# Product-key FFN block on one core: key search cut into pieces between weight splits, all up-weight splits on VectorE, larger gate-map instructions, streamed tiles at the right end of SBUF

## The chip, the core and the metric

One core of a Trainium2 chip runs the whole program. The metric is the device time of one execution in microseconds. Before the change it is 1149.65 us, the median of 3 runs (1148.85 to 1151.61).

## What is computed

One hybrid decoder layer for 256 tokens of width 1024 in float32: GLA and sparse attention from one input projection, cross-attention into 256 memory tokens, and then a PEER feed-forward block with 16,384 experts, with RMSNorms between. The front (both attentions, up to about 300 us) keeps its order; the change lies in the PEER block:

```
q = h @ Wq                               # 8 heads, two half keys each
s1, s2 = q1 @ subkeys1, q2 @ subkeys2    # 128 keys each
top-16 of s1, top-16 of s2               # values and ids
top-16 of (s1[a] + s2[b])                # over the 16 x 16 pairs
gate = softmax(top-16 scores)
expert = id1[a] * 128 + id2[b]
out = sum over the chosen: gate * gelu(h . down[expert]) * up[expert]
```

The kernel computes it densely: for every token the Gelu of all 16,384 experts, times a gate map that is zero where an expert is not chosen. An expert chunk is 128 experts with one second-key id; there are 128 chunks.

## The kernel before, in words

**Numbers as pairs.** Matmuls in fp32r lose bits, so every operand is a pair, a rounded high half and the remainder as a low half. `split` (L133 to L136) makes it: ScalarE copies the high half, VectorE, or GpSimd where the caller passes `P`, subtracts. `mm3` (L150 to L152) is then three matmuls: high by high, high by low, low by high. `weights` (L138) streams one chunk of 128 x 1024 floats by a DMA that SP issues into `raw` (4 buffers), and splits it into `whi` and `wlo` (3 buffers each), all of the pool `stream`.

**Two halves of 64 chunks.** Each half has a way down and a way back (loop `hf`, L852). *Way down*, per chunk `jj`: `proj_t` streams the down weights, splits them, and 24 matmuls (256 wide) fill a PSUM bank `pj` (2 of them); ScalarE writes the Gelu to `gl` (L862). *Way back*, per pair of chunks: the up weights are split, VectorE multiplies Gelu by the gate map (`L877`, 256 wide), the product is split into `Gh` and `Gl` (256 wide each), and 48 matmuls (512 wide) add to the four `y` banks.

**Who subtracts.** GpSimd makes the low halves of chunks 0 to 23 of the first half's way down (`LO_AT` 24) and of the first four chunks of each way back (`jj < 4`); VectorE makes the others.

**Key search.** While the first chunks run, VectorE finds the two top-16 lists (`best`, L734 and on) and the top-16 of the pairs. Then the loop at L772 turns positions into ids, per token tile `t` and key `q`: `idf` (ids as bf16), `past`, `ab`, `abf`, then a 2048-wide comparison `eq` (L789), its product with the ids broadcast over the 16 candidates (L791), four halving sums (L794) and a copy (L796). `gates_exp` (at chunk `EXP_AT`, 24) puts the `Exp` of the gates on ScalarE, `gates_t` (at chunk `KEY_AT`, 28) turns ids and gates to keys by tokens, and splits the gates into three bf16 parts `gp`.

**Gate maps.** From chunk 30 (`W_AT`) of the first half and chunk 8 of the second, two maps of 8 tokens come after every second chunk, 32 in a half (`gate_map`, L825). A map is two comparisons, `OI` (1024 wide) and `OJ` (512), three products `J` (L841), 24 short bf16 matmuls into a bank `pn` (2 of them), and a copy into `W` on ScalarE (L848).

**Order.** Nothing of the order is written out by hand. The framework's scheduler orders each engine's queue by its own estimates; `tc.issue_after(x)` holds an instruction behind `x`. An engine then works its queue strictly in that order, and waits for semaphores where an input or a buffer is late.

Of the kernel before, what the change touches and what calls it, by code (L numbers as in the profile page):

```python
# [23 lines left out]
HALF = NJ // 2  # L24


LO_AT, EXP_AT, KEY_AT, W_AT = 24, 24, 28, 30
SIZES = (256, 256, 512, 512, 16, 512, 128, 128, 128, 128, 128, 128, 24)
OFF = [0]
for _n in SIZES:  # L30
# [52 lines left out]
def body(ctx: ExitStack, tc, a, out, dbg=None):  # L83
# [49 lines left out]

    def split(src, hi, lo, eng=None):
        S.activation(hi, src, AF.Copy)  # L135
        (eng or V).tensor_sub(lo, src, hi.bitcast(FT))  # L136

    def weights(src, c, n, eng=None):  # L138

        raw = stream.tile([128, c * n], FT, name="raw", tag="raw", bufs=4)  # L140
        nc.sync.dma_start(raw, src)
        hi = stream.tile([128, c * n], FR, name="whi", tag="whi", bufs=3)
        lo = stream.tile([128, c * n], FR, name="wlo", tag="wlo", bufs=3)
        split(raw, hi, lo, eng)
        return hi.rearrange("p (c n) -> p c n", c=c), lo.rearrange("p (c n) -> p c n", c=c)
# [555 lines left out]
    def large(p):  # L701
        return p.tile([128, HALF, T], FT, name="big", tag="big")
# [4 lines left out]
    gp = [rt.tile([128, T], BF, name=f"gp{i}") for i in range(3)]  # L707
# [65 lines left out]
    for t in range(2):  # L773
        idf = ra.tile([128, 16, 16], BF, name="idf", bufs=2)
        V.tensor_copy(idf, ids[:, t])
        id4 = idf.rearrange("p (h q) k -> p h q k", q=2)
        past = ra.tile([128, 8, 16], U32, name="past", bufs=2)
        V.tensor_scalar(past, pos[t], 128, -128, op0=OP.max, op1=OP.add)
        for q in range(2):
            ab = ra.tile([128, 8, 16], U32, name="ab", bufs=2)  # L780
            if q == 0:
                V.tensor_scalar(ab, pos[t], 4, None, op0=OP.logical_shift_right)
            else:
                V.tensor_scalar(ab, pos[t], 15, None, op0=OP.bitwise_and)
            abf = ra.tile([128, 8, 16], BF, name="abf", bufs=2)
            V.tensor_tensor(abf, ab, past, op=OP.subtract if q else OP.add)
            eq = ra.tile([128, 8, 256], BF, name="eq", bufs=2)
            eq4 = eq.rearrange("p h (a k) -> p h a k", a=16)
            V.tensor_tensor(eq4, i16[:, None].to_broadcast([128, 8, 16, 16]),  # L789
                            abf[:, :, None, :].to_broadcast([128, 8, 16, 16]), op=OP.is_equal)  # L790
            V.tensor_tensor(eq4, eq4, id4[:, :, q, :, None].to_broadcast([128, 8, 16, 16]), op=OP.mult)  # L791
            for w in (128, 64, 32, 16):
                o = eq[:, :, :w]
                V.tensor_tensor(o, o, eq[:, :, w:2 * w], op=OP.add)  # L794
            r_ = ra.tile([128, 128], FT, name="r_", bufs=4)
            V.tensor_copy(r_.rearrange("p (h k) -> p h k", h=8), eq[:, :, :16])  # L796
            keys.append(r_)
# [10 lines left out]
    def gates_t(ins):  # L808
        p, pg = pn(), pn()
        with tc.issue_after(ins):  # L810
            for t in range(2):
                TE.transpose(p[:, t * 128:(t + 1) * 128], keys[2 * t], ident)
                TE.transpose(p[:, 256 + t * 128:256 + (t + 1) * 128], keys[2 * t + 1], ident)
                TE.transpose(pg[:, t * 128:(t + 1) * 128], g16[:, t].rearrange("p h k -> p (h k)"), ident)
        V.tensor_copy(idxi, p[:, :T])
        V.tensor_copy(idxj, p[:, T:])
        V.tensor_copy(gf, pg[:, :T])
        rr = ra.tile([128, T], FT, name="rr")
        V.tensor_copy(gp[0], gf)
        V.tensor_sub(rr, gf, gp[0])  # L820
        V.tensor_copy(gp[1], rr)
        V.tensor_sub(rr, rr, gp[1])
        V.tensor_copy(gp[2], rr)
        show("gf", gf)

    def gate_map(hf, W, t0):

        ts_ = slice(t0, t0 + 8)

        def two(x, n):  # L830
            return x[:, ts_].rearrange("p (g t) -> p g t", t=2)[:, :, None, :].to_broadcast([128, 4, n, 2])

        OI = rt.tile([128, 4, 128, 2], BF, name="OI", bufs=2)
        V.tensor_tensor(OI, ii2[:, None].to_broadcast([128, 4, 128, 2]), two(idxi, 128), op=OP.is_equal)
        OJ = rt.tile([128, 4, 64, 2], BF, name="OJ", bufs=2)
# [15 lines left out]
    big1 = None  # L851
    for hf in range(2):  # L852
        gl = g_half[hf]
        W = None
        for jj in range(HALF):
            j = hf * HALF + jj
            if hf == 0 and jj == EXP_AT:
# [5 lines left out]
            first = W_AT if hf == 0 else 8  # L863
            if jj % 2 and jj >= first and jj < first + 32:
                if W is None:
                    if hf == 0:
                        route.close()
                        big1 = pool(ctx, "big1")
                    W = large(big0 if hf else big1)
                for i in (jj - first - 1, jj - first):  # L870
                    gate_map(hf, W, i * 8)
        for jj in range(0, HALF, 2):
            G, w = [], []
            for i in range(2):
                j = hf * HALF + jj + i
                w.append(weights(a["up"][:, j], 1, D, P if jj < 4 else V))
                V.tensor_mul(gl[:, jj + i], gl[:, jj + i], W[:, jj + i])  # L877
                Gh = rt.tile([128, T], FR, name="Gh", bufs=2)
                Gl = rt.tile([128, T], FR, name="Gl", bufs=2)
                split(gl[:, jj + i], Gh, Gl)  # L880
                G.append((Gh, Gl))

            for i, t in ((0, 0), (1, 0), (0, 1), (1, 1)) if j == NJ - 1 else ((0, 0), (0, 1), (1, 0), (1, 1)):
# [93 lines left out]
```

## Time and profile before

| what | value |
|---|---|
| device time, median of 3 runs | 1149.65 us (1148.85 to 1151.61) |
| the profiled execution's own time | 1149.48 us |
| its span | 1147.7 us |
| PE (TensorE) busy | 1097.7 us, 96% |
| DVE (VectorE) busy | 812.9 us, 71% |
| ACT (ScalarE) busy | 580.9 us, 51% |
| POOL (GpSimd) busy | 157.0 us, 14% |
| mean granted TensorE clock | 0.982 |

The profile shows one execution, times in us from the span's start. A tile is given by the program's name without its buffer number; L136 is line 136 of the kernel. In a timeline, `x5` folds five instructions into one row, and the bracket gives the idle time ahead of it and what ended it. The granted clock is TensorE's, as a share of its full speed of 2.4 GHz. Matmuls overlap, so TensorE's pace is read from start to start.

### The profile page before, as it was taken

The page shows a single profiled execution, that of the slowest core. Times are in us where ns is not written, and L with a number is a line of the kernel's source. Part 1 is how long each engine was busy: PE and PEld are TensorE (multiplying, and loading weights), DVE is VectorE, ACT ScalarE, POOL GpSimd, SP SyncE. Part 2 cuts the span into 40 slices and gives each one's busy share as a digit, 9 for nine tenths or more (in the row PEclk, how much of TensorE's full clock was granted, in tenths as well). Part 3 has the DMA queues.
Part 4 walks back from the last instruction along what each step waited for, and adds up shares of the span by engine and source line. Part 5 has one row for each costly group of instructions (what it writes and reads, how often), then busy time and mean ns, then how long its engine had stood idle before and what let it go on. Part 6 is the DMA issues. An engine that isn't in the chain of part 4 may idle for free.

```text
span 1147.7 us, 20900 instructions
## 1 busy us (share of the span) xinstructions
PE 1097.7 (96%) x8174; PEld 979.4 (85%) x8174; DVE 812.9 (71%) x1698; ACT 580.9 (51%) x938; POOL 157.0 (14%) x83
## 2 busy tenths in 40 slices
PE   6999999999899969999799999999999999999996
PEld 5877789898799969999688888899999998888885
DVE  5763677675599978888786555547888956555555
ACT  5444445554454435666445444546666545445444
POOL 3303300000468900000500000000000003000001
PEclk9999999999899979999899999999999999999999
DMA  7633225563545535444365555564444565655653
GB/s 263 216 95 108 74 93 184 182 186 109 184 133 183 163 115 154 140 146 146 99 196 185 190 191 186 185 185 150 145 147 143 171 194 183 192 184 186 190 193 129
DMA packets 53568, 186.48 MB, mean 162 GB/s; under 512 B 6820, under 2 KB 8253, under 8 KB 53086
## 3 DMA queue, kind: packets, MB, share of 16 engines
q1 hardware_dynamic: 53470, 185.16, 51.1%
q8 instruction: 64, 1.05, 0.4%
q14 instruction: 34, 0.28, 0.1%
HBM read 182.76 MB, written 2.11 MB: 161 GB/s over the span
## 4 chain that ended last, share of the span: by engine, by line
PE 84%; DVE 11%; POOL 1%; DMA 1%; issue 1%; ACT 1%; SPq 0%; ACTq 0%; POOLq 0%; DVEq 0%
PE pj L150 13%; PE pj L151 13%; PE pj L152 13%; PE y L151 10%; PE y L152 10%; PE y L150 10%; PE pn L847 4%; PE po L152 1%; PE po L151 1%; PE po L150 1%; POOL wlo L136 1%; DVE eq L791 1%; DVE eq L794 1%; PE po L516 1%; DVE ids L734 1%
## 5 line engine op out<-in xcount | busy, mean ns | idle before, releaser
L135 ACT ACTIVATE whi<-raw 128x1024 fp32r<-128x1024 f32 (+1 forms) x328 | 344.3, 1050 | 287.4 <-PE pj L151 183.0
L136 DVE TENSOR_TENSOR wlo<-raw,whi 128x1024 fp32r<-128x1024 f32 x276 | 337.6, 1224 | 133.2 <-ACT whi L135 132.1
L152 PE MATMUL pj<-xh,wlo 128*128 128x256 f32 x1280 | 365.8, 286 | 12.6 <-DVE wlo L136 10.9
L150 PE MATMUL pj<-xh,whi 128*128 128x256 f32 x1280 | 369.4, 289 | 1.0 <-ACT tok L277 0.5
L151 PE MATMUL pj<-xl,whi 128*128 128x256 f32 x1280 | 365.3, 285 | 0.0
L152 PEld LDWEIGHTS pj<-xh,wlo 128*128 128x128 f32 x1280 | 247.7, 194 | 15.2 <-DVE wlo L136 11.4
L150 PEld LDWEIGHTS pj<-xh,whi 128*128 128x128 f32 x1280 | 247.6, 193 | 3.8 <-issue 0.9
L151 PEld LDWEIGHTS pj<-xl,whi 128*128 128x128 f32 x1280 | 247.8, 194 | 1.6 <-issue 1.0
L136 POOL TENSOR_TENSOR wlo<-raw,whi 128x1024 fp32r<-128x1024 f32 (+1 forms) x52 | 137.7, 2655 | 783.4 <-ACT whi L135 771.3
L151 PE MATMUL y<-wlo,Gh 128*128 128x512 f32 x512 | 203.6, 398 | 7.9 <-POOL wlo L136 7.9
L152 PE MATMUL y<-whi,Gl 128*128 128x512 f32 x512 | 203.4, 397 | 0.0
L150 PE MATMUL y<-whi,Gh 128*128 128x512 f32 x512 | 203.3, 397 | 0.0
L135 ACT ACTIVATE Gh<-big 128x256 fp32r<-128x256 f32 x128 | 53.3, 418 | 188.9 <-PE y L151 174.3
L151 PEld LDWEIGHTS y<-wlo,Gh 128*128 128x128 f32 x512 | 96.9, 189 | 31.6 <-POOL wlo L136 8.3
L150 PEld LDWEIGHTS y<-whi,Gh 128*128 128x128 f32 x512 | 96.8, 189 | 23.3
L152 PEld LDWEIGHTS y<-whi,Gl 128*128 128x128 f32 x512 | 96.8, 189 | 23.3
L136 DVE TENSOR_TENSOR Gl<-big,Gh 128x256 fp32r<-128x256 f32 x128 | 54.5, 427 | 77.6 <-ACT Gh L135 77.6
L841 DVE TENSOR_TENSOR J<-OJ,gp 128x512 bf16<-128x512 bf16 x192 | 74.9, 432 | 32.5 <-PE pn L847 32.5
L848 ACT ACTIVATE big<-pn 128x512 f32<-128x512 f32 x64 | 65.3, 1131 | 0.0
L877 DVE TENSOR_TENSOR big<-big 128x256 f32<-128x256 f32 x128 | 53.2, 466 | 3.3 <-ACT big L862 2.3
L847 PE MATMUL pn<-J,OI 128*128 128x64 bf16 x1536 | 52.1, 193 | 0.0
L847 PEld LDWEIGHTS <-OI 128*128 128x128 bf16 x1536 | 48.3, 97 | 1.4
(621 smaller groups left out, 1092.0 us busy)
## 6 DMA issues: line engine op xcount, KB each, us to landing
raw<-down_t SPq DMA_DIRECT2D x128, 512.0 KB, 3.8
raw<-up SPq DMA_DIRECT2D x128, 512.0 KB, 4.2
raw<-w_t SPq DMA_DIRECT2D x16, 512.0 KB, 4.4
raw<-xa_wk SPq DMA_DIRECT2D x8, 512.0 KB, 3.5
raw<-xa_wv SPq DMA_DIRECT2D x8, 512.0 KB, 3.8
raw<-w_out SPq DMA_DIRECT2D x8, 512.0 KB, 4.2
raw<-xa_wq SPq DMA_DIRECT2D x8, 512.0 KB, 3.9
raw<-xa_wo SPq DMA_DIRECT2D x8, 512.0 KB, 3.5
```

The costliest lines, as they stand in the source:

```text
L135: S.activation(hi, src, AF.Copy)
L136: (eng or V).tensor_sub(lo, src, hi.bitcast(FT))
L150: TE.matmul(o, lh, rh, start=start, stop=False)
L151: TE.matmul(o, lh, rl, start=False, stop=False)
L152: last["mm"] = TE.matmul(o, ll, rh, start=False, stop=stop)
L516: TE.matmul(pob[b][:, hd * 64:(hd + 1) * 64], pt_[:, i * 128:(i + 1) * 128], tok[:, k, b * 128 + g * 64:b * 128 + g * 64 + 64], start=k == ...
L734: V.max_index(ids[:, t, x, 8:], vals[:, t, x, 8:], s2_)
L791: V.tensor_tensor(eq4, eq4, id4[:, :, q, :, None].to_broadcast([128, 8, 16, 16]), op=OP.mult)
L841: V.tensor_tensor(J, OJ, two(gp[k], 64), op=OP.mult)
L847: TE.matmul(p[:, i], OI[:, g, :, q], Js[k][:, g, :, q], start=k == 0, stop=k == 2)
L848: S.activation(W[:, :, ts_].rearrange("p j t -> p t j"), p, AF.Copy)
L877: V.tensor_mul(gl[:, jj + i], gl[:, jj + i], W[:, jj + i])
```

## The change

1. **Key search in pieces.** GpSimd subtracts for chunks 0 to 19 only (`LO_AT` 20), and the search becomes a generator of 16 pieces. From chunk 20 on, each chunk issues one or two pieces, held behind the low half that was issued last, until chunk 32. `gates_exp` comes at chunk 21, `gates_t` at chunk 33 (`KEY_AT` 33). The ids are first written out 2048 wide by ScalarE (`rep`), so the product has two plain inputs.
2. **One J.** The three gate parts lie in one tile `gp` [128, T/8, 3, 8], and one product 1536 wide writes all three J's.
3. **Maps spread.** The 32 maps of a half are dealt out evenly, over 29 chunks from chunk 33 in the first half and over 54 from chunk 8 in the second. The first two maps of the second half are held behind the low half issued last.
4. **Way back.** VectorE splits all up weights. One product (512 wide) serves a pair of chunks and is held behind the low half issued last; `Gh` and `Gl` are one split of 512 per pair.
5. **Memory.** The pool `stream` moves to the right end of SBUF, with a margin of 8 floats behind it. The small `rstd` tiles have 2 buffers instead of 4.

The diff, cut to its core:

```diff
-LO_AT, EXP_AT, KEY_AT, W_AT = 24, 24, 28, 30
+LO_AT, KEY_AT = 20, 33
...
-    stream = pool(ctx, "stream")
+    edge = pool(ctx, "edge", side="right")
+    edge.tile([128, 8], FT, name="margin")
+    stream = pool(ctx, "stream", side="right")
...
-        (eng or V).tensor_sub(lo, src, hi.bitcast(FT))
+        last["lo"] = (eng or V).tensor_sub(lo, src, hi.bitcast(FT))
...
+    def key_pieces():
+        for t in range(2):
+            idf = ra.tile([128, 16, 16], BF, name="idf", bufs=2)
+            V.tensor_copy(idf, ids[:, t])
...
+                rep = ra.tile([128, 8, 256], BF, name="rep", bufs=2)
+                rep4 = rep.rearrange("p h (a k) -> p h a k", a=16)
+                S.activation(rep4, id4[:, :, q, :, None].to_broadcast([128, 8, 16, 16]), AF.Copy)
...
+                yield
...
-            V.tensor_tensor(eq4, eq4, id4[:, :, q, :, None].to_broadcast([128, 8, 16, 16]), op=OP.mult)
+                V.tensor_tensor(eq, eq, rep, op=OP.mult)
+                yield
...
-        Js = []
-        for k in range(3):
-            J = rt.tile([128, 4, 64, 2], BF, name=f"J{k}", bufs=2)
-            V.tensor_tensor(J, OJ, two(gp[k], 64), op=OP.mult)
-            Js.append(J)
+        J = rt.tile([128, 3, 4, 64, 2], BF, name="J", bufs=2)
+        parts = gp[:, t0 // 8].rearrange("p k (g t) -> p (k g) t", t=2)
+        V.tensor_tensor(J.rearrange("p k g j t -> p (k g) j t"),
+                        OJ.rearrange("p g j t -> p (g j t)")[:, None].to_broadcast([128, 3, 512]),
+                        parts[:, :, None, :].to_broadcast([128, 12, 64, 2]), op=OP.mult)
...
+            if hf == 0 and LO_AT <= jj < KEY_AT:
+                with tc.issue_after(last["lo"].ins):
+                    while done < 16 and done * (KEY_AT - 1 - LO_AT) < 16 * (jj + 1 - LO_AT):
+                        next(pieces)
+                        done += 1
+            first = KEY_AT if hf == 0 else 8
...
-                for i in (jj - first - 1, jj - first):
-                    gate_map(hf, W, i * 8)
+            while made < T // 8 and made * (HALF - 2 - first) < (T // 8) * (jj + 1 - first):
+
+                with tc.issue_after(last["lo"].ins) if hf and made < 2 else nullcontext():
+                    gate_map(hf, W, made * 8)
+                made += 1
...
-                w.append(weights(a["up"][:, j], 1, D, P if jj < 4 else V))
-                V.tensor_mul(gl[:, jj + i], gl[:, jj + i], W[:, jj + i])
...
+            with tc.issue_after(last["lo"].ins):
+                V.tensor_mul(g, g, v)
+            w = [weights(a["up"][:, hf * HALF + jj + i], 1, D, V) for i in range(2)]
+            G = [rt.tile([128, 2, T], FR, name=n, bufs=2) for n in ("Gh", "Gl")]
+            split(g, *G)
```

**VectorE at the key search.** Before, half of the search and the split behind it (`eq` comparison and product, `r_` the key, `wlo_4534` the low half of chunk 24; the four halving sums of L794 work on two tiles in turn):

```order
L791 TENSOR_TENSOR eq_3745<-eq_3745,idf_3724 128x2048
L794 TENSOR_TENSOR eq_3732<-eq_3732 128x8x128
L794 TENSOR_TENSOR eq_3745<-eq_3745 128x8x128
L794 TENSOR_TENSOR eq_3732<-eq_3732 128x8x64
L794 TENSOR_TENSOR eq_3745<-eq_3745 128x8x64
L794 TENSOR_TENSOR eq_3732<-eq_3732 128x8x32
L794 TENSOR_TENSOR eq_3745<-eq_3745 128x8x32
L794 TENSOR_TENSOR eq_3732<-eq_3732 128x8x16
L794 TENSOR_TENSOR eq_3745<-eq_3745 128x8x16
L796 CAST r__3739<-eq_3732 128x128
L796 CAST r__3752<-eq_3745 128x128
L136 TENSOR_TENSOR wlo_4534<-raw_4531,whi_4533 128x1024
```

Now, from the end of the top-16 (`g16`) on, with `wlo_4343`, `wlo_4392` and `wlo_4425` the low halves of chunks 20, 21 and 22:

```order
L773 TENSOR_TENSOR g16_3694<-top_3589 128x256
L138 TENSOR_TENSOR wlo_4343<-raw_4340,whi_4342 128x1024
L780 CAST idf_4372<-ids_3059 128x256
L783 TENSOR_SCALAR past_4374<-pos0_3590 128x128
L791 TENSOR_SCALAR ab_4378<-pos0_3590 128x128
L795 TENSOR_TENSOR abf_4380<-ab_4378,past_4374 128x128
L799 TENSOR_TENSOR eq_4382<-i16_3056,abf_4380 128x2048
L138 TENSOR_TENSOR wlo_4392<-raw_4389,whi_4391 128x1024
L802 TENSOR_TENSOR eq_4382<-eq_4382,rep_4376 128x2048
L138 TENSOR_TENSOR wlo_4425<-raw_4422,whi_4424 128x1024
L806 TENSOR_TENSOR eq_4382<-eq_4382 128x8x128
```

The search, two keys at a time in one block before, now goes one key at a time with a split after every piece or two, and the split of chunk 20 stands ahead of it.

**ScalarE at the same place.** `whi_4342`, `whi_4391`, `whi_4424`, `whi_4462` are the high halves of chunks 20 to 23; the rows of L878 are Gelus, `pj_4250` being chunk 17's and `pj_4346` chunk 20's:

```order
L137 ACTIVATE whi_4342<-raw_4340 128x1024
L878 ACTIVATE big_3048<-pj_4250 128x256
L788 ACTIVATE rep_4376<-idf_4372 128x2048
L878 ACTIVATE big_3048<-pj_4282 128x256
L137 ACTIVATE whi_4391<-raw_4389 128x1024
L788 ACTIVATE rep_4492<-idf_4372 128x2048
L878 ACTIVATE big_3048<-pj_4314 128x256
L137 ACTIVATE whi_4424<-raw_4422 128x1024
L137 ACTIVATE whi_4462<-raw_4460 128x1024
L878 ACTIVATE big_3048<-pj_4346 128x256
L814 ACT_TABLE_LOAD
L814 ACTIVATE g16_3694<-g16_3694 128x256
```

Two copies of 2048 (`rep`) and the `Exp` with its two table loads now stand among the high halves of chunks 20 to 23; the load back for the next Gelu follows the high half of chunk 24. Before, `Exp` stood at chunk 24.

**VectorE at the first turn.** Before, behind the last map's J and OI, up to the first up-weight split that VectorE makes (`wlo_7080`):

```order
L841 TENSOR_TENSOR J1_8785<-OJ_8781,gp1_3048 128x512
L841 TENSOR_TENSOR J2_8787<-OJ_8781,gp2_3049 128x512
L834 TENSOR_TENSOR OI_8815<-ii2_3050,idxi_3045 128x1024
L877 TENSOR_TENSOR big_3044<-big_3044,big_4808 128x256 x3
L136 TENSOR_TENSOR Gl_6993<-big_3044,Gh_6992 128x256
L136 TENSOR_TENSOR Gl_7004<-big_3044,Gh_7003 128x256
L877 TENSOR_TENSOR big_3044<-big_3044,big_4808 128x256 x18
L136 TENSOR_TENSOR Gl_7039<-big_3044,Gh_7038 128x256
L877 TENSOR_TENSOR big_3044<-big_3044,big_4808 128x256 x8
L136 TENSOR_TENSOR Gl_7050<-big_3044,Gh_7049 128x256
L877 TENSOR_TENSOR big_3044<-big_3044,big_4808 128x256
L136 TENSOR_TENSOR wlo_7080<-raw_7077,whi_7079 128x1024
```

Now, with `wlo_6838` the last down chunk's low half and `wlo_6871`, `wlo_6877`, `wlo_6912`, `wlo_6918` those of the first four up chunks:

```order
L854 TENSOR_TENSOR J_6775<-OJ_6773,gp_3051 128x1536
L138 TENSOR_TENSOR wlo_6838<-raw_6835,whi_6837 128x1024
L138 TENSOR_TENSOR wlo_6871<-raw_6868,whi_6870 128x1024
L901 TENSOR_TENSOR big_3048<-big_3048,big_4882 128x512
L138 TENSOR_TENSOR Gl_6881<-big_3048,Gh_6880 128x512
L901 TENSOR_TENSOR big_3048<-big_3048,big_4882 128x512
L138 TENSOR_TENSOR wlo_6877<-raw_6874,whi_6876 128x1024
L138 TENSOR_TENSOR Gl_6922<-big_3048,Gh_6921 128x512
L901 TENSOR_TENSOR big_3048<-big_3048,big_4882 128x512
L138 TENSOR_TENSOR wlo_6912<-raw_6909,whi_6911 128x1024
L138 TENSOR_TENSOR wlo_6918<-raw_6915,whi_6917 128x1024
```

The 18 and 8 products in a row are gone: products of 512 stand one at a time behind splits, and the splits of the first four up chunks have come to VectorE.

## Rows read from the trace of the kernel before

**Rows 1.** Table of stretches, all engines (first line: its columns).

```profile
core 0: us, PE busy (x) PEld busy (x) DVE busy (x) ACT busy (x) POOL busy (x), PEclk, DMA share, GB/s
400.00:420.00 20.00, 8.15 (x60) 7.75 (x60) 20.00 (x33) 5.69 (x8) 4.46 (x2) 0.75 0.21 61
500.00:520.00 20.00, 20.00 (x274) 19.87 (x273) 16.85 (x33) 13.03 (x18) 0.00 (x0) 1.00 0.52 149
```

**Rows 2.** TensorE's timeline, 397 to 424 us (start, us, engine, line, op, tiles, idle before).

```profile
397.33 0.39 PE L152 MATMUL pj<-xh,wlo 128*128 128x256 f32 x1 [0.38 <-POOL wlo L136]
...
401.71 0.39 PE L152 MATMUL pj<-xh,wlo 128*128 128x256 f32 x1 [1.25 <-POOL wlo L136]
...
407.45 0.28 PE L151 MATMUL pj<-xl,whi 128*128 128x256 f32 x1
...
418.33 0.58 PE L152 MATMUL pj<-xh,wlo 128*128 128x256 f32 x1 [10.60 <-DVE wlo L136]
...
423.57 0.28 PE L152 MATMUL pj<-xh,wlo 128*128 128x256 f32 x1
```

**Rows 3.** VectorE's timeline, the key search, and J in the map stretch.

```profile
390.52 8.90 DVE L791 TENSOR_TENSOR eq<-eq,idf 128x2048 bf16<-128x2048 bf16 x2
...
406.55 0.28 DVE L775 CAST idf<-ids 128x256 bf16<-128x256 uint32 x1
...
407.56 2.35 DVE L789 TENSOR_TENSOR eq<-i,abf 128x2048 bf16<-128x2048 bf16 x2
409.84 4.48 DVE L791 TENSOR_TENSOR eq<-eq,idf 128x2048 bf16<-128x2048 bf16 x2
...
417.06 3.48 DVE L136 TENSOR_TENSOR wlo<-raw,whi 128x1024 fp32r<-128x1024 f32 x3
...
542.14 1.09 DVE L841 TENSOR_TENSOR J<-OJ,gp 128x512 bf16<-128x512 bf16 x3
```

**Rows 4.** GpSimd's timeline, the last splits on the way down, and the turn.

```profile
383.42 2.54 POOL L136 TENSOR_TENSOR wlo<-raw,whi 128x1024 fp32r<-128x1024 f32 x1 [0.48 <-ACT whi L135]
386.30 18.16 POOL L136 TENSOR_TENSOR wlo<-raw,whi 128x1024 fp32r<-128x1024 f32 x5 [0.34 <-ACT whi L135]
...
561.24 10.73 POOL L136 TENSOR_TENSOR wlo<-raw,whi 128x1024 fp32r<-128x1024 f32 x1 [3.42 <-ACT whi L135]
```

**Rows 5.** TensorE's timeline, the turn.

```profile
563.51 0.40 PE L152 MATMUL y<-whi,Gl 128*128 128x512 f32 x1
563.74 0.39 PE L150 MATMUL y<-whi,Gh 128*128 128x512 f32 x1
572.02 0.79 PE L151 MATMUL y<-wlo,Gh 128*128 128x512 f32 x1 [7.89 <-POOL wlo L136]
...
577.22 0.40 PE L151 MATMUL y<-wlo,Gh 128*128 128x512 f32 x1
```

**Rows 6.** ScalarE's timeline, 388 to 411 us.

```profile
388.04 1.06 ACT L135 ACTIVATE whi<-raw 128x1024 fp32r<-128x1024 f32 x1 [1.55 <-issue]
...
408.80 1.28 ACT L801 ACT_TABLE_LOAD   x1
410.10 0.42 ACT L801 ACTIVATE g<-g 128x256 f32<-128x256 f32 x1
```

**Rows 7.** TensorE's timeline, a pair of maps between two chunks.

```profile
502.54 1.63 PE L847 MATMUL pn<-J,OI 128*128 128x64 bf16 x48
504.01 0.36 PE L150 MATMUL pj<-xh,whi 128*128 128x256 f32 x1
504.21 0.28 PE L151 MATMUL pj<-xl,whi 128*128 128x256 f32 x1
```

**Rows 8.** Costliest groups (busy us, mean ns of one | idle before): maps and G.

```profile
L848 ACT ACTIVATE big<-pn 128x512 f32<-128x512 f32 x64 | 65.3, 1131 | 0.0
L135 ACT ACTIVATE Gh<-big 128x256 fp32r<-128x256 f32 x128 | 53.3, 418 | 188.9 <-PE y L151 174.3
L877 DVE TENSOR_TENSOR big<-big 128x256 f32<-128x256 f32 x128 | 53.2, 466 | 3.3 <-ACT big L862 2.3
```

More of the change, by code (lines that the diff above doesn't have):

```diff
@@ L154, in rstd_of @@
     def rstd_of(late, early):
-        b, v, r, q = (tmp.tile([128, 1], FT, name=f"r{i}", tag=f"r{i}", bufs=4) for i in range(4))
+        b, v, r, q = (tmp.tile([128, 1], FT, name=f"r{i}", tag=f"r{i}", bufs=2) for i in range(4))
         V.tensor_scalar(b, early, 1.0 / D, EPS, op0=OP.mult, op1=OP.add)
@@ L706, in body @@
     idxj = rt.tile([128, T], BF, name="idxj")
-    gp = [rt.tile([128, T], BF, name=f"gp{i}") for i in range(3)]
+    gp = rt.tile([128, T // 8, 3, 8], BF, name="gp")
     ii2 = rt.tile([128, 128, 2], BF, name="ii2")
@@ L772, in body @@
     keys = []
[L773 to L790, printed above, removed]
-            V.tensor_tensor(eq4, eq4, id4[:, :, q, :, None].to_broadcast([128, 8, 16, 16]), op=OP.mult)
[L792 to L797, printed above, removed]
@@ new lines, in key_pieces @@
+    def key_pieces():
+        for t in range(2):
+            idf = ra.tile([128, 16, 16], BF, name="idf", bufs=2)
+            V.tensor_copy(idf, ids[:, t])
+            id4 = idf.rearrange("p (h q) k -> p h q k", q=2)
+            past = ra.tile([128, 8, 16], U32, name="past", bufs=2)
+            V.tensor_scalar(past, pos[t], 128, -128, op0=OP.max, op1=OP.add)
+            for q in range(2):
+                rep = ra.tile([128, 8, 256], BF, name="rep", bufs=2)
+                rep4 = rep.rearrange("p h (a k) -> p h a k", a=16)
+                S.activation(rep4, id4[:, :, q, :, None].to_broadcast([128, 8, 16, 16]), AF.Copy)
+                ab = ra.tile([128, 8, 16], U32, name="ab", bufs=2)
+                if q == 0:
+                    V.tensor_scalar(ab, pos[t], 4, None, op0=OP.logical_shift_right)
+                else:
+                    V.tensor_scalar(ab, pos[t], 15, None, op0=OP.bitwise_and)
+                abf = ra.tile([128, 8, 16], BF, name="abf", bufs=2)
+                V.tensor_tensor(abf, ab, past, op=OP.subtract if q else OP.add)
+                yield
+                eq = ra.tile([128, 8, 256], BF, name="eq", bufs=2)
+                eq4 = eq.rearrange("p h (a k) -> p h a k", a=16)
+                V.tensor_tensor(eq4, i16[:, None].to_broadcast([128, 8, 16, 16]),
+                                abf[:, :, None, :].to_broadcast([128, 8, 16, 16]), op=OP.is_equal)
+                yield
+                V.tensor_tensor(eq, eq, rep, op=OP.mult)
+                yield
+                for w in (128, 64, 32, 16):
+                    o = eq[:, :, :w]
+                    V.tensor_tensor(o, o, eq[:, :, w:2 * w], op=OP.add)
+                r_ = ra.tile([128, 128], FT, name="r_", bufs=4)
+                V.tensor_copy(r_.rearrange("p (h k) -> p h k", h=8), eq[:, :, :16])
+                keys.append(r_)
+                yield
@@ L818, in gates_t @@
         rr = ra.tile([128, T], FT, name="rr")
[L819 to L823, printed above, removed]
+        g8, r8 = (x.rearrange("p (g t) -> p g t", t=8) for x in (gf, rr))
+        V.tensor_copy(gp[:, :, 0], g8)
+        V.tensor_sub(r8, g8, gp[:, :, 0])
+        V.tensor_copy(gp[:, :, 1], r8)
+        V.tensor_sub(r8, r8, gp[:, :, 1])
+        V.tensor_copy(gp[:, :, 2], r8)
         show("gf", gf)
@@ L846, in gate_map @@
             for k in range(3):
-                TE.matmul(p[:, i], OI[:, g, :, q], Js[k][:, g, :, q], start=k == 0, stop=k == 2)
+                TE.matmul(p[:, i], OI[:, g, :, q], J[:, k, g, :, q], start=k == 0, stop=k == 2)
         S.activation(W[:, :, ts_].rearrange("p j t -> p t j"), p, AF.Copy)
@@ L851, in body @@
     big1 = None
+    pieces, done = key_pieces(), 0
     for hf in range(2):
@@ L854, in body @@
         W = None
+        made = 0
         for jj in range(HALF):
             j = hf * HALF + jj
-            if hf == 0 and jj == EXP_AT:
+            if hf == 0 and jj == LO_AT + 1:
                 gates_exp(gelu.ins)
@@ L862, in body @@
             gelu = S.activation(gl[:, jj], p, AF.Gelu_apprx_tanh)
[L863 to L869, printed above, removed]
-                for i in (jj - first - 1, jj - first):
-                    gate_map(hf, W, i * 8)
-        for jj in range(0, HALF, 2):
-            G, w = [], []
-            for i in range(2):
-                j = hf * HALF + jj + i
-                w.append(weights(a["up"][:, j], 1, D, P if jj < 4 else V))
-                V.tensor_mul(gl[:, jj + i], gl[:, jj + i], W[:, jj + i])
[L878 to L883, printed above, removed]
+            if hf == 0 and LO_AT <= jj < KEY_AT:
[3 more added lines that the diff above has]
+                        done += 1
@@ new lines, in body @@
+            first = KEY_AT if hf == 0 else 8
+            if jj < first:
+                continue
+            if W is None:
+                if hf == 0:
+                    route.close()
+                    big1 = pool(ctx, "big1")
+                W = large(big0 if hf else big1)
+            while made < T // 8 and made * (HALF - 2 - first) < (T // 8) * (jj + 1 - first):
+                with tc.issue_after(last["lo"].ins) if hf and made < 2 else nullcontext():
+                    gate_map(hf, W, made * 8)
+                made += 1
@@ new lines, in body @@
+        for jj in range(0, HALF, 2):
+            g, v = gl[:, jj:jj + 2], W[:, jj:jj + 2]
+            with tc.issue_after(last["lo"].ins):
[3 more added lines that the diff above has]
+            split(g, *G)
+            end = hf and jj == HALF - 2
+            for i, t in ((0, 0), (1, 0), (0, 1), (1, 1)) if end else ((0, 0), (0, 1), (1, 0), (1, 1)):
@@ L887, in body @@
                     n = slice(f * 512, (f + 1) * 512)
-                    mm3(y[t][f], G[i][0][:, s], G[i][1][:, s], w[i][0][:, 0, n], w[i][1][:, 0, n], j == 0, j == NJ - 1)
+                    mm3(y[t][f], G[0][:, i, s], G[1][:, i, s], w[i][0][:, 0, n], w[i][1][:, 0, n],
+                        j == 0, j == NJ - 1)
         if hf == 0:
```

## The prediction, made before the changed kernel was run

> **What bounds the kernel now.** I read four views in turn. The table of stretches comes first: in a normal stretch of the PEER loop TensorE is busy all 20 us at a granted clock of 1.00, but from 400 to 420 us only 8.15 of 20, at 0.75 [rows 1]. TensorE's timeline shows why: its last matmul before a hole starts at 407.45, and the next, at 418.33, is the first that needs the low half of chunk 24, which VectorE makes; two shorter waits, 0.38 and 1.25 us, were for GpSimd's low halves [rows 2]. Then the engines waited for. VectorE searches the keys without a break until 417.06 and only then splits chunk 24. The first half of the search runs beside GpSimd's splits, and there the two `eq` products take 8.90 us, against 4.48 in the second half, when GpSimd is done [rows 3]. GpSimd pays too: its last five splits take 18.16 us, where one took 2.54 before [rows 4]. At the turn to the way back one GpSimd split takes 10.73 us, beside a row of VectorE's products, and TensorE waits from 563.74 to 572.02 [rows 4, 5]. Elsewhere in the PEER part TensorE's own matmuls set the pace, so a lighter VectorE there is worth nothing by itself.
>
> **What the two holes cost.** Normally 47 steps take 401.71 to 407.45, 0.12 us each, so 24 matmuls, a chunk, take 2.88. First hole: 418.33 − 407.45 − 0.12 = 10.76 us of gap. Then the matmuls run at the lower of the clock's two levels, 1.2 GHz: the 24 steps from 418.33 to 423.57 take 5.24 us for 2.88, so 2.36 more. The two waits ahead are 0.38 and 1.25, and some 0.2 each for the restart (the stalled matmul lasts 0.39, a normal one 0.28, and the step after it is longer too). Together **15.2 us** [rows 2]. Second hole: a step is 0.23, so 572.02 − 563.74 − 0.23 = 8.05 us, and 12 steps to 577.22 take 5.20 for 2.8: **10.4 us** [rows 5]. That is 25.6 us, all that the change can win here.
>
> **The change part by part.**
> *Key search in pieces, LO_AT 24 to 20, KEY_AT 28 to 33.* GpSimd gives up chunks 20 to 23 and is done before 390, so the search no longer shares with it. VectorE's new order has the split of chunk 20 ahead of the search, so it stands idle from the end of the top-16 until ScalarE has made that chunk's high half, 388.04 + 1.06 = 389.1 [rows 6]. I count nothing for that; the room below pays it. Half of the search took 417.06 − 406.55 = 10.5 us alone. Its two products were 4.48 of that; both inputs are plain rows now (ScalarE writes `rep` out), so I price two between `is_equal`'s 2.35 and 4.48, at the first, which also reads plain rows of bf16: 8.4 us a half, 16.8 in all (21 at the other end) [rows 3]. The 13 splits of chunks 20 to 32 take 13 × 1.23 = 16 us (at most: three take 3.48) [rows 3], the gate sums 1.1. That is 34 us (38) in the 42 from 389.1 to TensorE's end of chunk 32: TensorE starts chunk 18 at 388.04, when the high half of chunk 20 may be written, so chunk 23 at 402.4 and chunk 33 at 431.2. A low half can be ready 5.76 − 1.06 − 1.23 = 3.5 us before its chunk, and no two splits have over 2.4 us of search between them (3.4 at the other end). So the first hole closes at either price.
> ScalarE gets four `rep` of 2048. Nearest row: 1.06 us for 1024 from SBUF, so 2.0; the other end, by the copy out of PSUM (1.13 for 512 [rows 8]), 4.5. The first two come right ahead of `Exp` and its table loads. Adding up ScalarE's order from 390.6, when `idf` is there: 2 × 2.0 for `rep`, 3 × 1.0 for high halves, 3 × 0.4 for Gelu (as `Exp`, also 256 wide) make 398.8; with load and `Exp` 1.70, a high half, the load back 1.28 and a Gelu, chunk 21's Gelu ends at 403.2 [rows 6]. TensorE wants that PSUM bank for chunk 23 at 402.4: **+0.8 us**, less than the 1.25 us after which the matmuls still kept their step. At the other end it is 5.8 us here and 2.5 at the second pair. The Trainium skill ("ScalarE: Activation LUTs", What ACT_TABLE_LOAD costs) counts a drain of about 1.38 us with each load. The trace has the load at 408.80 for 1.28 us and `Exp` at 410.10 [rows 6]: no drain. By the rule two loads would add 2.8 us here, and the sum would be 1130.6.
> *VectorE splits all on the way back; products in pairs, each held behind the last split.* The 26 products in two rows that stood ahead of the splits are gone from the order. At the turn the last map is copied to W within 1.7 us of TensorE's start of chunk 62 (high half, Gelu and 1.13 for the copy). Then product, high and low half of the first pair, at most two old ones each (0.93, 0.84, 0.93 [rows 8]): 4.4 us, against the 5.76 until the way back begins. So the second hole closes, with 1.3 us to spare. Steady: two splits 2.5, product and low half 1.9, 4.4 of the 24 × 0.23 = 5.6 us that a pair takes TensorE. That is the cover; if it is gone, each us more costs a us a pair.
> *One J for three, 512 to 1536.* Three took 1.09 us; one saves two starts, some 0.9 [rows 3]. VectorE's time, for which nobody waits: 0. Other end 1.68 us, at the old product's 1.09 ns an element (rival 1).
> *Maps spread.* First half: 32 maps in 29 chunks instead of 32; second: in 54. The matmuls are the same, but nearly every map now stands alone between chunks: 61 returns to the fp32r stream in place of 32 (three pairs remain). After a pair of maps the step from the first fp32r matmul to the next is 504.21 − 504.01 = 0.20 us, normally 0.12 [rows 7]: 0.08 × 29 = **+2.4 us**. At the start of the maps the first J follow the gate values so closely that TensorE waits some tenths at maps 1, 2 and 3: **+0.7** (0 to 1.5).
> *Streamed tiles at the right end, two `rstd` buffers for four.* In the front the order on every engine and its waits stay; no row shows an address to matter: 0. SP issues the same DMAs in the same order; 12 reloads wait for VectorE's split where they waited for GpSimd's.
>
> **Sum**, against the profiled execution's 1149.48 us (the runs' median is 1149.65, the same): 1149.5 − 15.2 − 10.4 + 0.8 + 2.4 + 0.7 = **1127.8 us**, my forecast.
>
> **Rivals.**
> 1. *J drops to one element a step.* VectorE then needs, per chunk of the first half, 1.23 + 1.1 × (2 × 0.36 + 0.36 + 1.68) = 4.3 us (`OI`, 1024 wide, as two J), 4.0 as starts overlap, against TensorE's 2.88 + 1.1 × (0.73 + 0.08) = 3.77 [rows 3, 7]: 0.25 × 29 = 7 us, **1135**. For: its operands are repeated over an outer dimension now. Against: inside they are the same pairs as before, and those ran at 0.36 us for 512. 0.07. The Trainium skill ("VectorE: DVE Perf Modes", Mode 2×_1P) asks for 16-bit data in unit steps; by that rule the rate stays.
> 2. *ScalarE falls behind*, `rep` at the PSUM copy's rate: 5.8 + 2.5 − 0.8 = 7.5 more, **1135**. For: a repeating input has no row. Against: the copies inside SBUF. 0.11.
> 3. *The turn's hole stays:* the first pair comes out of a chain over three engines with 1.3 us to spare. With the whole second hole kept, **1138**. 0.06.
> 4. *Slower:* TensorE's clock drops in the map stretches, where 61 groups of 0.03-us matmuls break the stream instead of 32. At 1.2 GHz 1 us of work loses 0.45 (2.88 for 5.24 [rows 2]). The stretches last 30 × 2.88 + 26 and 56 × 2.88 + 26, some 300 us; from 49 us at the lower level on the kernel is slower than before, and a fifth of them, 60 us, gives **1155**. Against: with the maps in pairs that stretch has 1.00 [rows 1]. 0.04. The Trainium skill ("TensorE: Matmul & The Clock Gate", A second HAM failure mode) tells of a kernel whose clock swings because the engine idles briefly between groups; by that rule this would happen.
>
> **Numbers.** Forecast 0.70, rivals 0.07, 0.11, 0.06 and 0.04, something else 0.02. The forecast's own span starts at 1123.9, if returns and new waits cost nothing, less 1.5 for the spread of runs (1148.85 to 1151.61), and ends at 1131. The range 1122 to 1135 takes in rivals 1 and 2 and leaves out 3 and 4. A measurement tells 0.3% (3.4 us) from no change: faster 0.94, same 0.02, slower 0.04.
>
> **What would show it.** Right: no TensorE wait over 1 us after 330 us and a clock of 1.00 from there on; GpSimd's last split before 390; `eq<-eq,rep` near 1.2 us, J near 0.9, `rep` near 2.0. Wrong: a wait of several us for a Gelu near 403, J above 1.6 and TensorE waiting for it, a wait on `Gl` at the turn, or a granted clock below 1.00 in the map stretches.

## The result and the profile after

The changed kernel takes 1105.05 us, the median of 4 runs (1102.04 to 1106.05); the kernel before took 1149.25 in the same comparison. The ratio is 0.961 (95% interval 0.958 to 0.964). The forecast was 1127.8 with a range of 1122 to 1135: the direction was right, the gain of 44 us twice the 22 forecast.

The page of the changed kernel (busy us and share of the span, and the chain that ended last):

```profile
span 1102.3 us, 20423 instructions
PE 1070.7 (97%) x8174; PEld 963.6 (87%) x8174; DVE 775.8 (70%) x1454; ACT 583.8 (53%) x878; POOL 113.9 (10%) x71
...
PE 92%; DVE 4%; ACT 1%; DMA 1%; issue 1%; SPq 0%; POOL 0%; ACTq 0%; DVEq 0%; POOLq 0%
```

TensorE's share of the chain has gone from 84 to 92%, VectorE's from 11 to 4%. Its table of stretches, where [rows 1] had 8.15 us of TensorE at a clock of 0.75:

```profile
400.00:420.00 20.00, 20.00 (x172) 20.00 (x172) 18.38 (x32) 12.69 (x16) 0.00 (x0) 1.00 0.60 180
500.00:520.00 20.00, 20.00 (x257) 19.79 (x257) 18.24 (x26) 12.79 (x17) 0.00 (x0) 1.00 0.41 133
...
330.00:1090.00 760.00, 758.58 (x6138) 695.88 (x6139) 548.62 (x850) 414.98 (x522) 44.30 (x18) 1.00 0.56 176
```

From 330 us to the end of the way back TensorE is idle for 1.4 us, at a clock of 1.00. What is left of waits there (us in total, times, longest); the second stands in the kernel before too, at 0.4 us:

```profile
PE pj L152 <- ACT big L878: 0.7, 1, 0.7
PE pn L726 <- ACT sc__3522 L728: 0.4, 1, 0.4
PE pn L861 <- DVE J L854: 0.2, 1, 0.2
```

Both holes are closed. VectorE's timeline at the search, against [rows 3]: a split stands between the pieces, and the product with `rep` takes 1.22 us where the broadcast one took 2.24 to 4.45.

```profile
386.94 1.22 DVE L802 TENSOR_TENSOR eq<-eq,rep 128x2048 bf16<-128x2048 bf16 x1
388.81 1.23 DVE L138 TENSOR_TENSOR wlo<-raw,whi 128x1024 fp32r<-128x1024 f32 x1 [0.66 <-ACT whi L137]
```

ScalarE's, against [rows 6], with one `rep` and the `Exp` between its two table loads:

```profile
385.66 1.90 ACT L788 ACTIVATE rep<-idf 128x2048 bf16<-128x2048 bf16 x1
...
390.01 1.28 ACT L814 ACT_TABLE_LOAD   x1
391.31 0.42 ACT L814 ACTIVATE g<-g 128x256 f32<-128x256 f32 x1
391.63 1.05 ACT L137 ACTIVATE whi<-raw 128x1024 fp32r<-128x1024 f32 x1
392.70 1.28 ACT L878 ACT_TABLE_LOAD   x1
393.99 0.38 ACT L878 ACTIVATE big<-pj 128x256 f32<-128x256 f32 x1
```

**What the holes don't explain.** In a stretch without any wait TensorE now makes more matmuls. Its row of the table of stretches, after (us, PE busy and starts, clock, DMA share, GB/s):

```profile
340.00:380.00 40.00, 40.00 (x355) 1.00 0.60 187
600.00:700.00 100.00, 100.00 (x443) 1.00 0.62 191
```

and in the kernel before:

```profile
340.00:380.00 40.00, 40.00 (x335) 1.00 0.56 175
600.00:700.00 100.00, 100.00 (x431) 1.00 0.59 189
```

Two of each count only reach into the stretch. By the distance from start to start, a 256-wide matmul of the way down takes 113.3 ns for 120.0, a 512-wide one of the way back 226.7 for 233.3, at the same clock. Two parts of the change could do this: the move of the streamed tiles, whose term I had put at nothing, or the fewer and wider instructions of the other engines beside TensorE.

### The profile page after: what moved, and what is told of

Read it like the earlier page. It is cut to its first block, busy times and chain, and to the rows that moved or that the text cites. A ratio compares the mean times of both kernels' runs of the same rounds, so it can differ in the third digit from the quotient of the medians.

```text
span 1102.3 us, 20423 instructions
## 1 busy us (share of the span) xinstructions
PE 1070.7 (97%) x8174; PEld 963.6 (87%) x8174; DVE 775.8 (70%) x1454; ACT 583.8 (53%) x878; POOL 113.9 (10%) x71
## 4 chain that ended last, share of the span: by engine, by line
PE 92%; DVE 4%; ACT 1%; DMA 1%; issue 1%; SPq 0%; POOL 0%; ACTq 0%; DVEq 0%; POOLq 0%
PE pj L152 15%; PE pj L153 15%; PE pj L154 15%; PE y L154 10%; PE y L153 10%; PE y L152 10%; PE pn L861 4%; PE po L152 1%; PE po L154 1%; PE po L153 1%; PE po L518 1%; PE pn L493 1%; PE pn L428 1%; PE pn L508 1%; DVE B L366 1%
## 5 line engine op out<-in xcount | busy, mean ns | idle before, releaser
L138 DVE TENSOR_TENSOR wlo<-raw,whi 128x1024 fp32r<-128x1024 f32 x288 | 352.2, 1223 | 186.7 <-ACT whi L137 185.6
L154 PE MATMUL pj<-xh,wlo 128*128 128x256 f32 x1280 | 360.1, 281 | 0.2 <-DVE wlo L138 0.2
L152 PEld LDWEIGHTS pj<-xh,whi 128*128 128x128 f32 x1280 | 241.5, 189 | 4.5 <-ACT big L878 1.2
L153 PEld LDWEIGHTS pj<-xl,whi 128*128 128x128 f32 x1280 | 241.5, 189 | 1.6 <-issue 1.0
L138 POOL TENSOR_TENSOR wlo<-raw,whi 128x1024 fp32r<-128x1024 f32 (+1 forms) x40 | 94.3, 2361 | 242.2 <-ACT whi L137 230.5
L137 ACT ACTIVATE Gh<-big 128x512 fp32r<-128x512 f32 x64 | 40.5, 632 | 87.5 <-PE y L153 85.9
L138 DVE TENSOR_TENSOR Gl<-big,Gh 128x512 fp32r<-128x512 f32 x64 | 44.3, 693 | 51.7 <-ACT Gh L137 51.7
L862 ACT ACTIVATE big<-pn 128x512 f32<-128x512 f32 x64 | 71.1, 1121 | 2.2 <-PE pn L861 2.2
L854 DVE TENSOR_TENSOR J<-OJ,gp 128x1536 bf16<-128x1536 bf16 x64 | 60.8, 951 | 0.0
L861 PE MATMUL pn<-J,OI 128*128 128x64 bf16 x1536 | 57.4, 194 | 0.3 <-DVE J L854 0.2
```

The lines of the kernel that those rows point to most:

```text
L138: last["lo"] = (eng or V).tensor_sub(lo, src, hi.bitcast(FT))
L152: TE.matmul(o, lh, rh, start=start, stop=False)
L153: TE.matmul(o, lh, rl, start=False, stop=False)
L154: last["mm"] = TE.matmul(o, ll, rh, start=False, stop=stop)
L854: V.tensor_tensor(J.rearrange("p k g j t -> p (k g) j t"), OJ.rearrange("p g j t -> p (g j t)")[:, None].to_broadcast([128, 3, 512]), part ...
L861: TE.matmul(p[:, i], OI[:, g, :, q], J[:, k, g, :, q], start=k == 0, stop=k == 2)
```

## The experiments

On the way down `whi` and `wlo` are stationary (the loaded weights of the matmul) and `xh` and `xl` move past them; on the way back `Gh` and `Gl` are stationary and `whi` and `wlo` move.

### Is it the address or the lighter traffic?

The edit of the first run: the streamed tiles go back to the left. The second makes the opposite edit in the kernel before.

```diff
-    edge = pool(ctx, "edge", side="right")
-    edge.tile([128, 8], FT, name="margin")
-    stream = pool(ctx, "stream", side="right")
+    stream = pool(ctx, "stream")
```

> The changed kernel with the pool of streamed weights back at the left end of SBUF, next to xh and xl (tiles begin at byte 33408 of a partition, a multiple of 128); everything else stays, and the order on every engine is the same. Theory PLACE (the address of the streamed tiles sets TensorE's step): the step of the 512-wide matmuls goes back from 226.6 to 233 ns and that of the 256-wide ones from 113 to 118 back to 120 ns; 1536 x 6.6 ns + some 3700 x 2.2 to 6.5 ns make 18 to 26 us, so 1123 to 1131 us. Rival TRAFFIC (the step is shorter because GpSimd and VectorE issue fewer and wider instructions beside it): the steps stay at 226.6 and 113 to 118, and the time at 1105.

> The kernel before with only its streamed tiles at the right end of SBUF, with the margin of 8 floats and two rstd buffers; order on every engine as before. PLACE: 512-wide steps go from 233 to 226.6 ns, 256-wide from 120 to 113 to 118; both holes (10.8 and 8 us waits) stay: 1149.3 - 18 to 26 = 1123 to 1131 us. TRAFFIC: 1149, steps at 233 and 120.

The two measured 1126.57 us (1123.97 to 1126.71) and 1123.81 (1123.49 to 1125.76). PLACE holds in both directions, TRAFFIC falls: the same instructions in the same order step at the old pace with the tiles at the left. The table of stretches of the first:

```profile
340.00:380.00 40.00, 40.00 (x334) 1.00 0.53 172
600.00:700.00 100.00, 100.00 (x430) 1.00 0.58 187
```

### The end of SBUF, or the offset?

A partition's small tiles (320 bytes) ahead of the streamed ones at the left, or behind them at the right, move these by 64 bytes within 128.

```diff
-    edge = pool(ctx, "edge", side="right")
-    edge.tile([128, 8], FT, name="margin")
-    stream = pool(ctx, "stream", side="right")
     tmp = pool(ctx, "tmp")
+    stream = pool(ctx, "stream")
```

```diff
     edge.tile([128, 8], FT, name="margin")
+    tmp = pool(ctx, "tmp", side="right")
     stream = pool(ctx, "stream", side="right")
-    tmp = pool(ctx, "tmp")
```

> The changed kernel with the streamed tiles at the left end, but behind the small tiles, so that they begin at byte 33728: 64 past a multiple of 128, as in the changed kernel at the right end. If the offset within 128 bytes is what counts (PLACE by offset): steps 226.6 and 113 to 118, 1105 us. If the end of SBUF is what counts (PLACE by region): steps 233 and 120, 1123 to 1131 us.

> The changed kernel with the streamed tiles at the right end, with the small tiles behind them, so that they begin at a multiple of 128 (byte 188032), as in the kernel before. By offset: steps 233 and 120, 1123 to 1131 us. By region: steps 226.6 and 113 to 118, 1105 us.

Measured: 1105.54 and 1116.23 us. The end of SBUF is not it: at the left with an offset of 64 the time is that of the changed kernel. But the second fell between the two expectations, since its 256-wide step went back and the 512-wide one did not (336 and 443 starts):

```profile
340.00:380.00 40.00, 40.00 (x336) 1.00 0.60 184
600.00:700.00 100.00, 100.00 (x443) 1.00 0.60 194
```

In that run `Gh` and `Gl` had moved too, to a multiple of 128. That suggested that the offset of the stationary tile against the moving one counts, and the next two were made for it: the small tiles ahead of `xh`, and a margin of 8 floats ahead of streamed tiles at the left.

```diff
+    tmp = pool(ctx, "tmp")
     keep = pool(ctx, "keep")
...
+    stream = pool(ctx, "stream")
```

```diff
-    edge = pool(ctx, "edge", side="right")
+    edge = pool(ctx, "edge")
     edge.tile([128, 8], FT, name="margin")
-    stream = pool(ctx, "stream", side="right")
+    stream = pool(ctx, "stream")
```

> The changed kernel with the small tiles first, then xh and xl, then the streamed tiles, all at the left end: xh, xl, whi, wlo, Gh and Gl all begin 64 past a multiple of 128. Theory RELATIVE (the 256-wide step is long when weights and moving rows begin at the same offset within 128 bytes, the 512-wide step when they differ by 64): 256-wide 120 ns, 512-wide 226.6, as in the run with the streamed tiles at a multiple of 128 at the right end, 1113 to 1119 us. Rival ABSOLUTE (a streamed tile must begin 64 past a multiple of 128): 256-wide 113 to 118, 512-wide 226.6, 1105 us.

> The changed kernel with the streamed tiles at the left end behind a margin of 32 bytes: xh begins at a multiple of 128, whi and wlo 32 past one, Gh and Gl 96 past one. RELATIVE: the 512-wide pair differs by 64, so 233 ns; the 256-wide pair differs by 32, anywhere from 113 to 120: 1115 to 1127 us. ABSOLUTE (only an offset of 64 helps): 233 and 120, 1126 us. If any offset other than a multiple of 128 helps: 226.6 and 113 to 118, 1105 us.

Measured: 1114.29 and 1122.95 us, steps of 120.0 and 226.7, and of 118.3 and 233.3: RELATIVE holds in both and ABSOLUTE in neither; the first run decides it, since for the second RELATIVE allowed any 256-wide step from 113 to 120. Two more looked at further differences (the first of them in the version with maps in pairs, below):

```diff
-    edge = pool(ctx, "edge", side="right")
+    edge = pool(ctx, "edge")
     edge.tile([128, 8], FT, name="margin")
```

```diff
-    edge = pool(ctx, "edge", side="right")
-    edge.tile([128, 8], FT, name="margin")
     stream = pool(ctx, "stream", side="right")
```

> The version with the maps in pairs, its streamed tiles without the margin at the right end and 32 bytes of margin behind xl instead: xh begins at a multiple of 128, whi, wlo, Gh and Gl all 96 past one; order on every engine as in the version with pairs. RELATIVE: the 512-wide pair still begins at the same offset, 226.6 ns. The 256-wide pair differs by 96: if 96 is as good as 64, 113 to 118 and 1100.5; if it keeps the step at 113 throughout, 2600 x 4.4 ns less, 1089 to 1095; if it is as bad as 0, 120 and 1108 to 1111 us.

> The changed kernel with its streamed tiles at the right end without the margin of 8 floats: whi and wlo begin 96 past a multiple of 128, xh at one, Gh and Gl 64 past one. RELATIVE: the 512-wide pair differs by 32: 226.6 ns if only a difference of 64 is bad, 233 if only 0 is good, something between if it goes by degrees; the 256-wide step as in the run above. 1105 where nothing changes, 1115 with 233. Rival MARGIN (the end of SBUF itself needs the margin): other engines' instructions on these tiles get longer too.

Measured: 1106.31 (1105.2 to 1107.72) and 1123.63 us. Neither is a time that I had named. The first lies between its branches: at a difference of 96 the 256-wide step averages 117.5 to 117.9 ns in each stretch of the way down, not 113. The second has the 512-wide step of 233.3, and is 8 us above the 1115 that goes with it: its 256-wide step is also longer than in the changed kernel, and 120.0 from 758 us on, so that its second way down takes 210.3 us for 207.6. MARGIN falls: VectorE's split of a chunk stays at 1224 ns; what the margin does here is to set the offset. All runs together; the offsets are the tiles' first bytes within 128, by the program's allocation, the steps mean ns from start to start in 340 to 380 and 600 to 700 us, without gaps:

| run | xh, whi, Gh | 256-wide: whi less xh, step | 512-wide: whi less Gh, step |
|---|---|---|---|
| before | 0, 0, 64 | 0: 120.0 | 64: 233.3 |
| after | 0, 64, 64 | 64: 113.3 | 0: 226.7 |
| before, tiles at the right | 0, 64, 64 | 64: 113.3 | 0: 226.7 |
| after, left | 0, 0, 64 | 0: 120.0 | 64: 233.3 |
| after, left, 64 on | 0, 64, 64 | 64: 117.8 | 0: 226.7 |
| after, right, 0 | 0, 0, 0 | 0: 120.0 | 0: 226.7 |
| after, xh at 64 too | 64, 64, 64 | 0: 120.0 | 0: 226.7 |
| after, left, 32 on | 0, 32, 96 | 32: 118.3 | 64: 233.3 |
| pairs, all 96 on | 0, 96, 96 | 96: 117.3 | 0: 226.7 |
| after, no margin | 0, 96, 64 | 96: 118.7 | 32: 233.3 |

For the 512-wide step a difference of 0 is good, 32 and 64 are bad. For the 256-wide one 0 is bad, and the others are better in this stretch; the last row's 96 is as bad as 0 from 758 us on. By the same allocation every difference of 0 in the table is one of 0 within 512 bytes too; no run has 128, 256 or 384, so that the pattern repeats every 128 bytes is not shown.

### The other parts, one by one

Key search in one block again, in the changed kernel (in short):

```diff
-LO_AT, KEY_AT = 20, 33
+LO_AT, KEY_AT = 24, 33
...
-    pieces, done = key_pieces(), 0
+    for _ in key_pieces():
+        pass
```

> The changed kernel with the key search of the kernel before: one block on VectorE ahead of the low half of chunk 24, the product with the ids broadcast, GpSimd subtracting up to chunk 23, Exp at chunk 24; the gate maps still begin at chunk 33. Forecast's theory (the search in one block is what kept TensorE waiting): the wait of some 10.8 us and the matmuls at 1.2 GHz behind it come back, + 15.2 - 0.8 us: 1105 + 14 = 1119 (1117 to 1121). Rival (with the streamed tiles moved, the search alone was not the limit): 1105 to 1109.

Measured 1119.6 us (1118.61 to 1122.32): the hole is back, as expected.

```profile
PE pj L154 <- DVE wlo L138: 11.4, 1, 11.4
PE pj L154 <- POOL wlo L138: 2.2, 2, 1.4
```

The whole way back as before, and then only GpSimd's four splits:

```diff
-            with tc.issue_after(last["lo"].ins):
-                V.tensor_mul(g, g, v)
...
+                w.append(weights(a["up"][:, j], 1, D, P if jj < 4 else V))
+                V.tensor_mul(gl[:, jj + i], gl[:, jj + i], W[:, jj + i])
```

```diff
-            w = [weights(a["up"][:, hf * HALF + jj + i], 1, D, V) for i in range(2)]
+            w = [weights(a["up"][:, hf * HALF + jj + i], 1, D, P if jj < 4 else V) for i in range(2)]
```

> The changed kernel with the way back of the kernel before: GpSimd subtracts for the first four chunks, products and G 256 wide, products not held back. Forecast's theory (GpSimd's split is starved beside a row of VectorE's products): the wait for a low half at the turn, 8 us, and 12 matmuls at 1.2 GHz come back: 1105 + 10 = 1115 (1113 to 1117). Rival (steady pairs also gain from the wider instructions): more than 1117, with TensorE waiting in the steady part of the way back.

> The changed kernel with GpSimd subtracting for the first four chunks of each way back, as before, but products 512 wide and held, as after. If the row of products starved GpSimd: its splits take 2.4 to 5 us, no wait over 2 us at the turn, 1105 to 1107 us. If GpSimd is too slow beside VectorE's splits as well: a wait of some 8 us at the turn, 1113 to 1117 us.

Measured 1121.95 us (1121.69 to 1122.65) and 1103.78 (1103.14 to 1106.95). The first costs 17 us where 10 were expected: one of GpSimd's splits comes late at each turn (7.4 and 5.9 us), where the kernel before had a hole at the first turn alone. TensorE waits nowhere else on the way back, so the rival for the steady part did not come.

```profile
PE y L153 <- POOL wlo L138: 13.2, 2, 7.4
```

VectorE's row of products at the first turn (in two pieces, a split of `G` between them):

```profile
536.58 6.79 DVE L903 TENSOR_TENSOR big<-big 128x256 f32<-128x256 f32 x20
...
543.62 2.42 DVE L903 TENSOR_TENSOR big<-big 128x256 f32<-128x256 f32 x7
```

GpSimd's three splits from there on, and the first of them alone:

```profile
537.13 15.77 POOL L138 TENSOR_TENSOR wlo<-raw,whi 128x1024 fp32r<-128x1024 f32 x3 [2.09 <-ACT whi L137]
```

```profile
537.13 11.12 POOL L138 TENSOR_TENSOR wlo<-raw,whi 128x1024 fp32r<-128x1024 f32 x1 [2.09 <-ACT whi L137]
```

The row ends at 546.04, the first split 2.2 us later, and the other two take 2.36 us each. In the second run, with products 512 wide and held, the three take half of that, and TensorE waits for none of them:

```profile
536.49 8.19 POOL L138 TENSOR_TENSOR wlo<-raw,whi 128x1024 fp32r<-128x1024 f32 x3 [2.24 <-ACT whi L137]
```

So the new form of the products, wider and held, is what closes the second hole; wider products without the hold were not run. That VectorE took GpSimd's splits adds nothing that can be measured.

Three J again:

```diff
-        V.tensor_tensor(J.rearrange("p k g j t -> p (k g) j t"),
...
+        for k in range(3):
+            V.tensor_tensor(J[:, k], OJ, parts[:, 4 * k:4 * k + 4, None, :].to_broadcast([128, 4, 64, 2]), op=OP.mult)
```

> The changed kernel with three J products of 512 in place of one of 1536. Forecast (nobody waits for J): 1105, J 3 x 0.36 us. Rival (VectorE is short of time in the first map stretch, where J stands ahead of the low halves): 1106 to 1109, with waits for wlo or J.

Measured 1105.26 us (1104.79 to 1110.27): the same, though VectorE works longer, 3 x 416 ns a map against 951:

```profile
L855 DVE TENSOR_TENSOR J<-OJ,gp 128x512 bf16<-128x512 bf16 x90 | 32.6, 416 | 0.0
```

Maps in pairs:

```diff
                     gate_map(hf, W, made * 8)
-                made += 1
+                    gate_map(hf, W, made * 8 + 8)
+                made += 2
```

> The changed kernel with its gate maps dealt out in pairs (16 places in a half instead of 32). Forecast's term (each return from the bf16 matmuls of a map costs 0.08 us; some 29 fewer returns): 1105.05 - 2.4 = 1102.7. Rival 1 (TensorE takes no longer for single maps): 1105. Rival 2 (pairs crowd VectorE and ScalarE, TensorE waits for J or a PSUM bank): 1106 to 1110. Beside it: if the 256-wide step of 113 or 118 ns is chosen by where the maps break the stream, the step of the first map stretch goes from 118 to 113, another 3 us less.

Measured 1100.5 us (1098.6 to 1101.99), a ratio to before of 0.958 (0.957 to 0.960): the lowest of all. It is 4.5 us under the changed kernel; the two spreads just miss each other (1101.99 and 1102.04). The traces, below, give 3.2 of them to the stretches with maps. The step of 113 came for a part of the first map stretch: 117.8 from 441 to some 497 us, 113.4 from there to the way back.

## Why the prediction was wrong, and where it was right

The start-to-start times of the traces, by stretch (us; the limits are the first and last starts of the 512-wide matmuls):

| stretch | before | after, tiles at the left | after | pairs |
|---|---|---|---|---|
| start to first way back | 560.94 | 546.96 | 537.77 | 535.54 |
| first way back | 189.42 | 178.97 | 173.85 | 173.87 |
| second way down | 209.18 | 210.56 | 207.59 | 205.68 |
| second way back | 178.97 | 178.97 | 173.85 | 173.85 |

The second column is the change without its address, the third adds the address.

- **The step that failed: "no row shows an address to matter: 0".** Between the second and third columns lie 9.2 + 5.1 + 3.0 + 5.1 = 22.4 us, and 1126.57 − 1105.05 = 21.5 between the medians. On the way back that is 1536 matmuls at 6.6 ns, 10.2 us; the rest is the 256-wide steps. I gave a term for which I had no row the value nothing, without bounds. A row could have warned me: at a clock of 1.00 a 512-wide matmul started every 0.23 us [rows 5], while 512 columns over 2.4 GHz are 0.213. I took TensorE's step as fixed because it did not wait. The Trainium skill ("TensorE: Matmul & The Clock Gate", Step-by-step) says that loading the next weights takes no SBUF bandwidth from the running matmul; by that rule this term is 0. It measured 21.5 us: the step of these fp32r matmuls depends on where the stationary tile begins against the moving one. Whether the weight load is what meets the running matmul, no run shows.
- **First hole, 15.2, right.** To the first way back the second column saves 14.0 us; my terms for that part were 15.2, less 0.8, 0.7 and half of 2.4, that is 12.5, and in that run neither the 0.8 nor the 0.7 was lost: 12.5 + 1.5 = 14.0. Undoing the pieces alone, in the changed kernel, cost 14.6 us, as expected.
- **Second hole, 10.4, right:** 189.42 − 178.97 = 10.45 us.
- **`rep` and the table loads, +0.8: the right wait, its size by luck.** `rep` took 1.90 us, and TensorE waited once, 0.73 us, for the Gelu behind `Exp`. But the 0.8 was worked out for a step of 0.12 us, and in the run that has that step, with the tiles at the left, the wait is gone (its Gelu ended at 401.80, not 403.2): the shorter step brought it. The Trainium skill ("ScalarE: Activation LUTs", What ACT_TABLE_LOAD costs) counts a drain with a load; here each load is followed at once by its instruction (390.01 + 1.28, then 391.31), so no drain shows.
- **Maps spread, +2.4, right.** Both with steps of 120.0, the kernel before and the change with its tiles at the left differ by 1.38 us on the second way down, for 16 more returns: 0.086 each, where I had 0.08. In the changed kernel the first step after a map is 0.201 us for 0.118. With maps in pairs, from the first map (430.98 us; 430.03 with pairs) to the first way back 106.79 − 105.51 = 1.3 us are saved, and on the second way down 1.9. Of these 3.2 us the 27 fewer returns make 2.2, some 310 matmuls that step at 113 in place of 118 there make 1.4, which I had not foreseen, and waits for J take some tenths back.
- **First J's, +0.7, too high:** one wait of 0.2 us, and none with the tiles at the left. **One J, 0, right.**
- Rivals 1 to 4 did not come: J at 0.95 us, ScalarE's wait of 0.73, no wait at the turn, a clock of 1.00.

The forecast of 1127.8 us is thus within 1.3 us of the change without its address, 1126.57.

## What to carry to other kernels

Before a tuned kernel's busiest engine is taken as fixed, compare its step with columns over clock: what is above that may be room, and a busy share of 100% doesn't show it. Here 6.6 of the 20 ns above it were, for the 512-wide matmuls. An edit that moves data to other addresses gets a term with bounds, not a nothing. Here the first bytes of the stationary and the moving tile within 128 bytes were worth 21 us of 1127, for a few lines of code; try both offsets for each pair of tiles.

## What the runs showed of the hardware

- **Step and offset.** With no engine waiting and a clock of 1.00, fp32r steps differ by 6.6 to 6.7 ns with the offsets in the table above, at both widths. That is the time of 16 columns at 2.4 GHz, or 64 bytes of a row. What lengthens the step, and why 512 columns want a difference of 0 and 256 columns another, no run shows.
- **Two paces at one offset.** At a difference of 64 the 256-wide step is 113.3 or 117.8 ns, in one and the same execution. In the changed kernel it is 113.3 until TensorE's pause at 393.42, 117.8 until the transposes of the keys at 422.8, 113.3 again after them, and after some changes among the first maps 117.8 from 443 us on (matmuls in 25 and in 6 us):

```profile
397.00:422.00 25.00, 25.00 (x215) 1.00 0.61 192
424.00:430.00 6.00, 6.00 (x55) 1.00 0.23 80
```

In the eight traces with this difference the pace never changes within an unbroken row of 256-wide matmuls of the PEER block. All 35 changes found lie across a break in the row (a pause, the transposes, a map, a turn), and most breaks change nothing. Nor does a break push one way: at its wait for the same Gelu (396.82) the run with the tiles 64 on at the left goes from 117.8 to 113.3. What picks the pace was not found; 4.4 ns over the some 2,300 matmuls that run at 117.8 in the changed kernel would be some 10 us.

```profile
393.42 0.28 PE L154 MATMUL pj<-xh,wlo 128*128 128x256 f32 x1
394.43 0.39 PE L152 MATMUL pj<-xh,whi 128*128 128x256 f32 x1 [0.73 <-ACT big L878]
```

- **GpSimd beside VectorE.** A GpSimd split takes 2.40 us alone and 2.56 to 2.86 where VectorE's products come one at a time. Beside a dense row of them it gets next to nothing done: in the run with the old way back splits took 11.12 and 10.52 us at the two turns, in the kernel before 10.73 [rows 4], and each of the three ended 2.2 us after the last product of the row, nearly a whole split later.
